# Fewer weight subtractions on GpSimd, and a hand-written VectorE order in a convolution's norm

## The chip, the cores and the metric

The kernel runs on one core of a Trainium2 chip. The metric is the device time of one execution in microseconds (us). Before the change three runs took 630.7, 631.92 and 632.24 us (median 631.92). The profile comes from one more execution, which took 633.2 us.

## The reference, cut to what matters

Two layers of a decoder trunk work on x of 256 rows x 1024, in float32. Layer 0 is an RMS norm, one projection (1024 to 3072) for two attention mixers of eight heads each, an output projection, a residual, an RMS norm and a SwiGLU feed-forward of width 2816. Layer 1 has the same frame with other mixers:

```python
gz, ca, cg = split(rms_norm(x) @ odd_w_in + odd_b_in)
gu, gv = split(gelu(gz)); gv = layer_norm(gv)      # gMLP: gv mixed over rows per group
c_out = gu * (tril(w_s) @ gv + b_s)
c = ca * sigmoid(cg)                               # Conformer convolution, 512 channels, 31 taps
c = causal_depthwise_conv(c, conv_w) + conv_b
d_out = silu(layer_norm(c))                        # the norm that the change reorders
x = x + concat(c_out, d_out) @ odd_w_out
x = x + swiglu(rms_norm(x))
```

## The kernel before, in words

**Split products.** Every float32 product is made of three TensorE passes: each operand is split into a rounded high half and the rest (low). For activations the helper `split` does it (lines 239, 240). For weights it is done once per block.

**Weight blocks.** The weights are cut into blocks of 1 MB, in the order of use: `dk dq dv mk mq mv` (two blocks of four rows of tiles each, attention's projections), `eo` (four, output projection), feed-forward 0, then layer 1: `gv` (two), `cg ca cg ca` (numbers 0, 0, 1, 1), `gu` (two), `oo` (four: 0, 2, 4, 6), feed-forward 1. A `Block` has two halves `f`. Each half takes two steps: `split_hi`, a copy on ScalarE (tile `whi`, line 133), and `split_lo`, a subtraction raw - high (tile `wlo`, line 137) on VectorE, or on GpSimd where the block was planned so. In attention these are `mv` 0, `dv` 1 and `mq` 1 (`ON_POOL`); in layer 1 `cg`, `ca`, `gu` and `oo`, except `oo` 4.

**When they are issued.** Using a block for the first time puts the steps of the one two places on into the list `todo` (`ahead`; the pair `cg`, `ca` together). `pump(n)` issues the next n steps; `tick`, called from every matmul step, pumps one at a set pace unless `held`. After the second half's `split_lo` a block calls `load_next`: SyncE's queue issues the load of the block three places on, into the raw buffer that has come free (three raw buffers, eight buffers each for high and low halves).

**Order.** TensorE runs in the order of the program. The other engines' order is set by a planner when the program is built, except inside regions opened by `in_order(...)`, where the named engines run in the order written. GpSimd's order in the convolution stage is written (`pool_order`).

**Attention.** `qk_prep` norms and rotates a projection (lines 607 to 631); a power on GpSimd (line 620) gives its factors. A unit (a pair of heads) has a start (scores, line 700; mask and maximum on VectorE, line 707; exponentials on ScalarE, 709), for the differential heads `dc` (745) and `e` (747) on VectorE, then two units later the transposes of `e` on TensorE (718), and after that the product with v (728). Projection steps fill TensorE between units.

**Norm between stages (`close`).** The last products of rows 0 to 127 (m = 0), then those of m = 1, are ended by residual (358) and sum of squares; `norm_rows` gets the factor (a power on GpSimd, 310) and scales two halves of the row (`scr`, line 331); `norm_T` transposes them on TensorE (340) and splits them. The transposes of m = 1 stand between the first steps of the next stage. Steps of the weight blocks are pumped at three places, their numbers in `SPLITS`: in the norm of m = 0, after its first transpose, and in the norm of m = 1. Entry 1 is the `close` ahead of layer 1.

**Convolution's norm.** The mean over channels is a matmul with ones (1172). Per m: `center` subtracts it (1177), squares on ScalarE (1180), sums over the four channel tiles on VectorE (1182). `scale` sums over partitions on TensorE (1188), takes the power on GpSimd (299), and makes a scaled identity `dg` (1192). `conv_out` spreads it with a matmul (1197), multiplies (1198), applies SiLU on ScalarE (1201) and splits the result into `cT` (shown as `oT` in the profile). Between them `some(n)` runs n of the sixteen ready steps of the output projection (`SOME`), and the rest runs after. The products that need the convolution's part come after that, in `close`.

Of the kernel before, what the change touches and what calls it, by code (L numbers as in the profile page):

```python
# [22 lines left out]
F32 = mybir.dt.float32  # L23
FR = mybir.dt.float32r
AF = mybir.ActivationFunctionType
ALU = mybir.AluOpType
AX = mybir.AxisListType

P = 128
# [3 lines left out]
MT = S // P  # L33
# [9 lines left out]
LOOK = 2  # L43
PACE = (3, 1, 2, 1)

ON_POOL = (('mv', 0), ('dv', 1), ('mq', 1))

WARM = (5, 4)
PUMPS = (0, 9, 7)

# [7 lines left out]
SHARES = (5, 4, 4, 5, 4, 1, 7, 5, 1, 1, 5, 4, 0, 1, 5, 0, 3, 2, 2, 7, 2)  # L58


SPLITS = ((2, 3, 7), (12, 3, 1), (7, 3, 5))
N_T0 = (5, 4, 5)
N_T1 = (10, 5, 10)


TAP_RATE = 0.55
N_DIAG = 12
SOME = (3, 4, 2, 4)
LAMBDA_INIT = 0.8 - 0.6 * math.exp(-0.3 * 0)


# [1 line left out]
def trunk_kernel(ctx: ExitStack, tc: tile.TileContext, a: dict, out: bass.AP):  # L73
    nc = tc.nc
# [11 lines left out]
    def scratch():  # L86
        return act.tile([P, 512], F32, name="scr", tag="scr", bufs=6)
# [8 lines left out]
    plan, blocks, todo = [], {}, deque()  # L96
    at_block, ticks, held, background, pace = [-1], [0], [False], [], [PACE[0]]

    class Block:


        def __init__(self, src, rows_, cols, axis, lo_engine):
            self.src, self.rows, self.cols, self.axis = src, rows_, cols, axis
            self.lo_engine = lo_engine or nc.vector
            self.per = rows_ // 2
            self.parts, self.left = [None, None], [1, 1]
            self.index, self.loaded, self.pair = len(plan), False, None
# [26 lines left out]

        def split_lo(self, f, r=slice(None)):
            hi, lo = self.half(f)
            self.lo_engine.tensor_tensor(lo[:, r], self.source(f)[:, r], hi[:, r].bitcast(F32), op=ALU.subtract)  # L137

        def split_row(self, i, lo_engine):

            f, r = i // self.per, slice(i % self.per, i % self.per + 1)
            self.split_hi(f, r)
            self.lo_engine = lo_engine
            self.split_lo(f, r)
            self.left[f] = 0
            if i == self.rows - 1:
                self.load_next()
# [25 lines left out]
    def pump(n):  # L173
        for _ in range(min(n, len(todo))):
            b, f, step = todo.popleft()
            step(f)
            if step == b.split_lo:
                b.left[f] = 0
                if f == 1:
                    b.load_next()  # L180
# [10 lines left out]
    def plan_w(key, src, k0, kn, c0, cn, axis="k", lo_engine=None):  # L191
        b = Block(src[k0 * P:(k0 + kn) * P, c0:c0 + cn].rearrange("(k p) n -> p k n", p=P), kn, cn, axis, lo_engine)
        plan.append(b)
        blocks[key] = b

    def plan_out(name, src, nk, **kw):
        for k0 in range(0, nk, 2):
            plan_w((name, k0), src, k0, 2, 0, D, **kw)

    def plan_ffn(layer):  # L200
        for j in range(FT // 2):
            for part in range(2):
                plan_w((f"f{layer}", j, part), a["ffn_w_in"][layer], 0, KT, part * FF + j * 256, 256, "c" if j else "k")
        plan_out(f"fo{layer}", a["ffn_w_out"][layer], FT)

    for name, c0 in (("dk", 512), ("dq", 0), ("dv", 1024), ("mk", 2048), ("mq", 1536), ("mv", 2560)):
        for h in range(2):
            plan_w((name, h), a["even_w_in"][0], 4 * h, 4, c0, 512, lo_engine=nc.gpsimd if (name, h) in ON_POOL else None)
    plan_out("eo", a["even_w_out"][0], KT)
    plan_ffn(0)  # L210
    for h in range(2):
# [5 lines left out]
    for j in range(2):  # L217
        plan_w(("gu", j), a["odd_w_in"][0], 0, KT, j * 256, 256, "c", lo_engine=nc.gpsimd)
    plan_out("oo", a["odd_w_out"][0], KT, lo_engine=nc.gpsimd)
    blocks["oo", 4].lo_engine = nc.vector  # L220
    plan_ffn(1)

    def passes(ps, lhs, rhs, first, last):
# [13 lines left out]
    def split(hi, lo, src):  # L237

        nc.scalar.activation(hi, src, AF.Copy)
        nc.vector.tensor_tensor(lo, src, hi.bitcast(F32), op=ALU.subtract)  # L240

    def in_order(*engines):

        region = ExitStack()
        region.enter_context(tc.manual_schedule(engines={getattr(mybir.EngineType, e) for e in engines}))
        return region
# [5 lines left out]
    ident = consts.tile([P, P], F32, name="ident")  # L252
# [26 lines left out]
    def col(name, i):  # L279
        return vec[:, rows[name] + i:rows[name] + i + 1]  # L280
# [14 lines left out]
    def rsqrt_mean(dst, ss, n, width):  # L295

        t = small.tile([P, width], F32, name="ms", tag=f"ms{width}")
        nc.vector.tensor_scalar(t, ss, 1.0 / n, EPS, op0=ALU.mult, op1=ALU.add)
        nc.gpsimd.tensor_tensor(dst, t, neg_half[:, :width], op=ALU.pow)
# [24 lines left out]
    def norm_rows(m, ss, gB, splits):  # L324

        r = row_factor(ss)
        pump(splits)
        xn = []
        for n in range(2):
            xn.append(scratch())  # L330
            nc.vector.scalar_tensor_tensor(xn[n], xs[:, m, n * 512:(n + 1) * 512], r, gB[:, n * 512:(n + 1) * 512],  # L331
                                           op0=ALU.mult, op1=ALU.mult)
        return xn

    def norm_T(m, n, xn, xT, ptag):

        pt = ptag()
        ms = slice(m * P, (m + 1) * P)
        for j in range(4):
            nc.tensor.transpose(pt[:, j * P:(j + 1) * P], xn[n][:, j * P:(j + 1) * P], ident)  # L340
        split(xT[0][:, 4 * n:4 * n + 4, ms], xT[1][:, 4 * n:4 * n + 4, ms], pt.rearrange("p (a b) -> p a b", b=P))

    def run(steps):
        for _ in steps:
            pass
# [17 lines left out]
    def tail_steps(lhs, ws, k0, m, pss, order):  # L363

        for n, k in order:
            out_step(lhs, ws[k // 2], k0 + k, k % 2, m, n, pss[m][n], False, k == 3)
            yield n, k
# [4 lines left out]
    def close(site, lhs, ws, k0, pss, gB, ptag, tail0=True):  # L372
# [5 lines left out]
        def end(m, n):  # L378
            residual(m, n, pss)
            square(m, n, ss[m])  # L380
# [9 lines left out]
        end(0, 1)  # L390
        xn0 = norm_rows(0, ss[0], gB, SPLITS[site][0])
        for i, (n, k) in enumerate(tail_steps(lhs, ws, k0, 1, pss, BY_BLOCK)):
            if i == 3 and ws[0].index + 4 < len(plan):
                plan[ws[0].index + 4].ahead()
            if i == N_T0[site]:
                norm_T(0, 0, xn0, xT, ptag)
                pump(SPLITS[site][1])
            if k == 3:
                end(1, n)
        norm_T(0, 1, xn0, xT, ptag)  # L400
        xn1 = norm_rows(1, ss[1], gB, SPLITS[site][2])

# [85 lines left out]
    with tc.tile_pool(name="attn", bufs=1) as ap, tc.tile_pool(name="pat", bufs=1, space=bass.MemoryType.PSUM) as pat:  # L488
# [242 lines left out]
        class DiffPair:  # L731
            late = LAG + 3
# [29 lines left out]
        class MobaPair:  # L762
            late = LAG + 2
# [136 lines left out]
        for m in range(MT):  # L900
            po = pat.tile([P, 512], F32, name="po", tag="po")
            r = ap.tile([P, 2, NH // 2, 2], F32, name="dr", tag="dr", bufs=2)
            units += [DiffPair(m, p, po, r) for p in range(4)]
        for m in range(MT):
            po = pat.tile([P, 512], F32, name="po", tag="po")
            r = ap.tile([P, NH // 2, 2], F32, name="mr", tag="mr", bufs=2)
# [94 lines left out]
    with tc.tile_pool(name="odd", bufs=1) as op, tc.tile_pool(name="pod", bufs=1, space=bass.MemoryType.PSUM) as pod:  # L1001
# [168 lines left out]
        def mean():  # L1170
            for i, ct in enumerate((3, 0, 1, 2)):
                nc.tensor.matmul(pm[:, :S], ones, conv[:, ct, :], start=i == 0, stop=i == 3)

        def center(m):
            ms = slice(m * P, (m + 1) * P)
            cm[m] = scratch().rearrange("p (a b) -> p a b", b=P)
            nc.vector.scalar_tensor_tensor(cm[m], pm[:, None, ms].to_broadcast([P, 4, P]), -1.0 / 512, conv[:, :, ms],
                                           op0=ALU.mult, op1=ALU.add)
            csq = scratch().rearrange("p (a b) -> p a b", b=P)
            nc.scalar.activation(csq, cm[m], AF.Square)  # L1180
            csum = scratch()[:, :P]
            nc.vector.tensor_reduce(csum, csq.rearrange("p a b -> p b a"), axis=AX.X, op=ALU.add)
            return csum

        def scale(m, csum):

            var = pm[:, S + m:S + m + 1]
            nc.tensor.matmul(var, csum, ones[:, 0:1], start=True, stop=True)
            rs = small.tile([P, 1], F32, name="cvr")
            rsqrt_mean(rs, var, 512, 1)  # L1190
            dg = scratch()[:, :P]
            nc.vector.tensor_scalar(dg, ident, rs, None, op0=ALU.mult)
            return dg

        def conv_out(m, dg):
            ms = slice(m * P, (m + 1) * P)
            nc.tensor.matmul(pb[:, ms], ones, dg, start=True, stop=True)
            nc.vector.tensor_tensor(cm[m], cm[m], pb[:, None, ms].to_broadcast([P, 4, P]), op=ALU.mult)
            dT = scratch().rearrange("p (a b) -> p a b", b=P)
            for ct in range(4):  # L1200
                nc.scalar.activation(dT[:, ct, :], cm[m][:, ct, :], AF.Silu, scale=col("cln_g", ct), bias=col("cln_b", ct))
            split(cT[0][:, 4:, ms], cT[1][:, 4:, ms], dT)
# [15 lines left out]
        def some(n):  # L1218
            for _ in range(n):
                next(part)  # L1220

        some(SOME[0])
        mean()
        csum = [center(m) for m in range(MT)]
        some(SOME[1])
        dg = [scale(0, csum[0])]
        some(SOME[2])
        dg.append(scale(1, csum[1]))
        conv_out(0, dg[0])
        some(SOME[3])  # L1230
        conv_out(1, dg[1])
        run(part)
        pool_order.close()
        ws = [blocks["oo", k0] for k0 in (4, 6)]
# [65 lines left out]
```

## Time and profile before

| | |
|---|---|
| profiled execution | 633.2 us; span of its instructions 631.4 us |
| TensorE matmul busy | 609.0 us, 96% of the span |
| weight load on TensorE (beside matmuls) | 517.6 us, 82% |
| VectorE busy | 421.1 us, 67% |
| ScalarE busy | 345.7 us, 55% |
| GpSimd busy | 121.7 us, 19% |
| `wlo` on VectorE, line 137 | 166 instructions, 206.3 us |
| `wlo` on GpSimd, line 137 | 26 instructions, 62.9 us |
| DMA | 104.32 MB, mean 165 GB/s |
| granted TensorE clock, mean | 0.989 |

How to read it: an engine's busy time is the sum of its instructions; an instruction that is held up while it runs counts as busy. The granted clock is a share of full speed; 1.00 is 2.4 GHz, 0.50 is 1.2 GHz. "idle before <- releaser" names the instruction that ended last among those that were waited for. Times in windows and timelines count from the start of the span.

### The profile page before, as it was taken

The numbers are of one execution on the slowest core, as the hardware profiler recorded it, in microseconds if no ns is written. First come the engines' busy times: TensorE is split into PE (matmuls) and PEld (weight loads), VectorE is DVE, ScalarE is ACT, GpSimd is POOL, SyncE is SP. The second block draws the span as 40 slices with busy tenths as digits, with TensorE's granted clock in tenths as the row PEclk, the third lists the DMA queues.
The fourth block names the chain that finished last, engine by engine and source line by source line (L and its number), as shares of the span: only waits on it lengthen the run. The fifth ranks groups of instructions, "written<-read, shape, count | busy, mean of one in ns | idle before, by whom it ended". The sixth has DMA issues, their size and how long they took to land.

```text
span 631.4 us, 8906 instructions
## 1 busy us (share of the span) xinstructions
PE 609.0 (96%) x3420; PEld 517.6 (82%) x3420; DVE 421.1 (67%) x710; ACT 345.7 (55%) x621; POOL 121.7 (19%) x97
## 2 busy tenths in 40 slices
PE   7989799999999999999998999988999999999997
PEld 5867577787988888888886899867988888888886
DVE  3799998547666648664446389986766666665431
ACT  5764686555655587553446775446455555554320
POOL 1998321101000000000003695550000000000000
PEclk9999799999999999999999799999999999999999
DMA  7855424224766437555552553225656555555401
GB/s 248 308 196 175 158 106 132 70 66 149 245 225 215 146 128 266 185 168 185 199 197 67 167 199 134 68 89 178 208 193 201 196 174 173 193 199 190 145 0 67
DMA packets 72791, 104.32 MB, mean 165 GB/s; under 512 B 3068, under 2 KB 56492, under 8 KB 72748
## 3 DMA queue, kind: packets, MB, share of 16 engines
q1 hardware_dynamic: 72748, 103.74, 49.5%
q8 instruction: 27, 0.44, 0.3%
q14 instruction: 16, 0.13, 0.1%
HBM read 102.69 MB, written 1.05 MB: 164 GB/s over the span
## 4 chain that ended last, share of the span: by engine, by line
PE 52%; issue 29%; DVE 11%; POOL 3%; ACT 2%; DMA 1%; SPq 1%; POOLq 0%; DVEq 0%; ACTq 0%
PE mm L233 15%; PE mm L225 8%; PE mm L227 8%; PE mm L234 8%; PE mm L226 8%; DVE wlo L137 3%; DVE scr L331 2%; PE tq L700 1%; DMA raw<-in_even_w_in 1%; POOL rm L310 1%; DVE t L627 1%; PE po L728 1%; ACT whi L133 1%; DVE t L621 1%; PE tq L718 1%
## 5 line engine op out<-in xcount | busy, mean ns | idle before, releaser
L133 ACT ACTIVATE whi<-raw 128x1024 fp32r<-128x1024 f32 (+1 forms) x192 | 197.7, 1040 | 175.7 <-PE mm L233 80.1
L137 DVE TENSOR_TENSOR wlo<-raw,whi 128x1024 fp32r<-128x1024 f32 (+1 forms) x166 | 206.3, 1248 | 124.5 <-ACT whi L133 122.9
L233 PE MATMUL mm<-xT,whi 128*128 128x512 f32 x640 | 226.8, 399 | 0.0
L234 PE MATMUL mm<-xT,wlo 128*128 128x256 f32 x640 | 179.7, 281 | 0.0
L233 PEld LDWEIGHTS mm<-xT,whi 128*128 128x128 f32 x640 | 120.2, 188 | 29.6 <-issue 0.2
L234 PEld LDWEIGHTS mm<-xT,wlo 128*128 128x128 f32 x640 | 120.9, 189 | 0.0
L225 PE MATMUL mm<-whi,xT 128*128 128x512 f32 (+1 forms) x176 | 68.2, 387 | 0.6 <-ACT xT L545 0.5
L137 POOL TENSOR_TENSOR wlo<-raw,whi 128x1024 fp32r<-128x1024 f32 (+1 forms) x26 | 62.9, 2439 | 19.7 <-ACT whi L133 19.6
L227 PE MATMUL mm<-whi,hT_lo 128*128 128x512 f32 (+1 forms) x176 | 66.5, 378 | 0.0
L226 PE MATMUL mm<-wlo,hT_hi 128*128 128x512 f32 (+1 forms) x176 | 66.5, 378 | 0.0
L225 PE MATMUL mm<-whi,hT_hi 128*128 128x512 f32 (+1 forms) x176 | 66.4, 378 | 0.0
L227 PE MATMUL mm<-whi,xT 128*128 128x512 f32 (+1 forms) x176 | 64.1, 364 | 1.1 <-DVE xT L240 1.1
L226 PE MATMUL mm<-wlo,xT 128*128 128x512 f32 (+1 forms) x176 | 64.3, 366 | 0.5 <-DVE wlo L137 0.5
L310 POOL TENSOR_TENSOR rm<-st,neg_half 128x1 f32<-128x1 f32 x8 | 7.1, 894 | 188.9 <-DVE st L308 188.9
L225 PEld LDWEIGHTS mm<-whi,xT 128*128 128x128 f32 x176 | 34.5, 196 | 7.8 <-issue 1.6
L227 PEld LDWEIGHTS mm<-whi,xT 128*128 128x128 f32 x176 | 34.6, 196 | 6.8 <-DVE xT L240 1.8
L226 PEld LDWEIGHTS mm<-wlo,xT 128*128 128x128 f32 x176 | 34.7, 197 | 4.8 <-DVE wlo L137 1.3
L225 PEld LDWEIGHTS mm<-whi,hT_hi 128*128 128x128 f32 x176 | 33.1, 188 | 6.4
L226 PEld LDWEIGHTS mm<-wlo,hT_hi 128*128 128x128 f32 x176 | 33.1, 188 | 6.4
L227 PEld LDWEIGHTS mm<-whi,hT_lo 128*128 128x128 f32 x176 | 33.0, 188 | 6.4
L464 DVE TENSOR_TENSOR scr<-mm,scr 128x256 f32<-128x256 f32 x80 | 33.2, 418 | 5.8 <-ACT scr L463 5.7
L1077 DVE SCALAR_TENSOR_TENSOR cv<-cpad,cw,cv 128x256 f32<-128x256 f32 x87 | 35.7, 481 | 0.2
(226 smaller groups left out, 868.6 us busy)
## 6 DMA issues: line engine op xcount, KB each, us to landing
raw<-in_ffn_w_in SPq DMA_DIRECT2D x44, 1024.0 KB
raw<-in_ffn_w_out SPq DMA_DIRECT2D x22, 1024.0 KB
raw<-in_even_w_in SPq DMA_DIRECT2D x10, 1024.0 KB
raw<-in_odd_w_in SPq DMA_DIRECT2D x8, 1024.0 KB
raw<-in_even_w_out SPq DMA_DIRECT2D x4, 1024.0 KB
raw<-in_odd_w_out SPq DMA_DIRECT2D x4, 1024.0 KB
xs<-in_x SPq DMA_DIRECT2D x4, 256.0 KB
raw<-in_even_w_in SPq DMA_DIRECT2D x4, 256.0 KB
```

Of the source, the lines that this page charges most:

```text
L133: nc.scalar.activation(self.half(f)[0][:, r], self.source(f)[:, r], AF.Copy)
L137: self.lo_engine.tensor_tensor(lo[:, r], self.source(f)[:, r], hi[:, r].bitcast(F32), op=ALU.subtract)
L225: nc.tensor.matmul(ps, lhs[0], rhs[0], start=first, stop=False)
L226: nc.tensor.matmul(ps, lhs[0], rhs[1], start=False, stop=False)
L227: nc.tensor.matmul(ps, lhs[1], rhs[0], start=False, stop=last)
L233: nc.tensor.matmul(bank, w[0], x[2][:, k, :, :].rearrange("p a b -> p (a b)"), start=k == 0, stop=False)
L234: nc.tensor.matmul(bank[:, :S], w[1], x[0][:, k, :], start=False, stop=k == KT - 1)
L310: nc.gpsimd.tensor_tensor(r, t[:, 1:2], neg_half[:, :1], op=ALU.pow)
L331: nc.vector.scalar_tensor_tensor(xn[n], xs[:, m, n * 512:(n + 1) * 512], r, gB[:, n * 512:(n + 1) * 512], op0=ALU.mult, op1=ALU.mult)
L464: nc.vector.tensor_tensor(s, bank[:, :S], s, op=ALU.add)
L621: nc.vector.scalar_tensor_tensor(t1v, psv, rx[m], c, op0=ALU.mult, op1=ALU.mult)
L1077: nc.vector.scalar_tensor_tensor(conv[:, ct, :] if t == TAPS - 1 else acc, cpad[:, ct, t:t + S], cw[:, t, ct:ct + 1], acc, op0=ALU.mult, o ...
```

## The change

The list `ON_POOL` goes: all attention blocks subtract on VectorE. A block now has one engine for each half; of `cg` 0 and `ca` 0 the second half goes to VectorE. `SPLITS` entry 1 pumps one step more after the first transpose and none in the norm of m = 1. In the convolution's norm VectorE runs in the order written; both `center` come before both sums; `dg` is made on ScalarE; the SiLU and the split are a function of their own, called after both products; the high halves of `oo` 4 and 6 are issued ahead of the norm and their low halves at set places (`oo` 4 on VectorE, `oo` 6 on GpSimd).

```diff
-ON_POOL = (('mv', 0), ('dv', 1), ('mq', 1))
...
-SPLITS = ((2, 3, 7), (12, 3, 1), (7, 3, 5))
+SPLITS = ((2, 3, 7), (12, 4, 0), (7, 3, 5))
...
-SOME = (3, 4, 2, 4)
+SOME = (3, 4, 1, 2, 1)
...
-            self.lo_engine = lo_engine or nc.vector
+            self.lo_engine = [lo_engine or nc.vector] * 2
...
-            self.lo_engine.tensor_tensor(lo[:, r], self.source(f)[:, r], hi[:, r].bitcast(F32), op=ALU.subtract)
+            self.lo_engine[f].tensor_tensor(lo[:, r], self.source(f)[:, r], hi[:, r].bitcast(F32), op=ALU.subtract)
...
-            plan_w((name, h), a["even_w_in"][0], 4 * h, 4, c0, 512, lo_engine=nc.gpsimd if (name, h) in ON_POOL else None)
+            plan_w((name, h), a["even_w_in"][0], 4 * h, 4, c0, 512)
...
-    blocks["oo", 4].lo_engine = nc.vector
+    for b in (blocks["cg", 0], blocks["ca", 0]):
+        b.lo_engine[1] = nc.vector
+    blocks["oo", 4].lo_engine = [nc.vector] * 2
...
             nc.scalar.activation(csq, cm[m], AF.Square)
+            return csq
+
+        def summed(csq):
             csum = scratch()[:, :P]
...
-            nc.vector.tensor_scalar(dg, ident, rs, None, op0=ALU.mult)
+            nc.scalar.activation(dg, ident, AF.Copy, scale=rs)
...
             nc.vector.tensor_tensor(cm[m], cm[m], pb[:, None, ms].to_broadcast([P, 4, P]), op=ALU.mult)
+
+        def conv_silu(m):
+            ms = slice(m * P, (m + 1) * P)
             dT = scratch().rearrange("p (a b) -> p a b", b=P)
...
+        late = [blocks["oo", k0] for k0 in (4, 6)]
+        for b in late:
+            for f in range(2):
+                b.left[f] = 2
+                b.split_hi(f)
+
+        def low(b, f):
+            b.split_lo(f)
+            b.left[f] = 0
+            if f == 1:
+                b.load_next()
+
+        order = in_order("DVE")
         some(SOME[0])
         mean()
-        csum = [center(m) for m in range(MT)]
+        low(late[0], 0)
+        low(late[1], 0)
+        csq = [center(m) for m in range(MT)]
+        csum = [summed(c) for c in csq]
         some(SOME[1])
         dg = [scale(0, csum[0])]
         some(SOME[2])
         dg.append(scale(1, csum[1]))
+        some(SOME[3])
         conv_out(0, dg[0])
-        some(SOME[3])
+        some(SOME[4])
         conv_out(1, dg[1])
+        low(late[0], 1)
+        low(late[1], 1)
+        for m in range(MT):
+            conv_silu(m)
+        order.close()
         run(part)
```

## Rows read from the trace of the kernel before

**Rows 1.** Windows: us, busy PE, PEld, DVE, ACT, POOL (instructions); clock, DMA, GB/s.
```profile
31.20:63.50 32.30, 30.43 (x148) 23.53 (x146) 32.30 (x53) 17.46 (x30) 29.01 (x10) 1.00 0.55 186
63.50:67.14 3.64, 0.04 (x2) 0.00 (x1) 3.57 (x5) 1.46 (x3) 3.18 (x2) 1.00 0.57 230
67.14:74.50 7.36, 7.36 (x25) 5.75 (x26) 7.32 (x29) 5.22 (x17) 1.64 (x1) 0.54 0.37 142
...
85.00:97.00 12.00, 11.98 (x75) 9.27 (x76) 12.00 (x37) 9.74 (x27) 2.74 (x2) 1.00 0.26 88
...
344.95:347.80 2.85, 0.10 (x2) 0.03 (x1) 2.85 (x2) 1.40 (x5) 2.85 (x2) 0.96 0.00 0
347.80:354.40 6.60, 6.29 (x23) 5.18 (x24) 4.56 (x4) 3.95 (x12) 4.85 (x2) 0.50 0.39 111
...
415.10:422.10 7.00, 5.34 (x24) 3.89 (x24) 5.39 (x9) 2.09 (x3) 4.17 (x4) 1.00 0.49 152
422.10:427.20 5.10, 3.14 (x13) 2.13 (x14) 5.10 (x5) 3.79 (x8) 1.63 (x1) 1.00 0.46 141
```
**Rows 2.** TensorE's waits, whole span: us in total, times, longest us.
```profile
PE tq L718 <- DVE e L747: 3.6, 1, 3.6
PE cv L340 <- DVE scr L331: 3.1, 2, 2.7
PE mm L227 <- DVE oT_lo L240: 1.9, 1, 1.9
```
**Rows 3.** Timeline of GpSimd in attention: start us, us, instruction.
```profile
32.10 5.93 POOL L137 TENSOR_TENSOR wlo<-raw,whi 128x1024 fp32r<-128x1024 f32 x2
...
52.02 5.36 POOL L137 TENSOR_TENSOR wlo<-raw,whi 128x1024 fp32r<-128x1024 f32 x2
...
61.53 5.14 POOL L137 TENSOR_TENSOR wlo<-raw,whi 128x1024 fp32r<-128x1024 f32 x2
```
**Rows 4.** Timeline of VectorE in attention.
```profile
31.22 4.56 DVE L137 TENSOR_TENSOR wlo<-raw,whi 128x1024 fp32r<-128x1024 f32 x2
...
52.70 2.35 DVE L873 TENSOR_TENSOR lsum<-lexp 128x1 f32<-128x1 f32 x1
...
55.05 3.41 DVE L137 TENSOR_TENSOR wlo<-raw,whi 128x1024 fp32r<-128x1024 f32 x1
...
62.24 2.23 DVE L627 TENSOR_TENSOR t<-t,rsh 128x512 f32<-128x512 f32 x1
...
64.60 2.10 DVE L745 SCALAR_TENSOR_TENSOR dc<-sums,neg_lam,dr 128x2 f32<-128x2 f32 x1
...
80.38 0.18 DVE L743 RECIPROCAL dr<-sums 128x4 f32<-128x4 f32 x1 [1.09 <-ACT e L709]
```
**Rows 5.** Single lines, whole span: duration ns min/median/max, first and last start us.
```profile
L137 DVE TENSOR_TENSOR wlo<-raw,whi x166: 678/1226/3429, 6.1 to 606.9; 128x1024 fp32r<-128x1024 f32 x160, 128x512 fp32r<-128x512 f32 x6
L627 DVE TENSOR_TENSOR t<-t,rsh x4: 680/1462/2271, 36.3 to 74.2; 128x512 f32<-128x512 f32 x4
L745 DVE SCALAR_TENSOR_TENSOR dc<-sums,neg_lam,dr x8: 211/214/2099, 64.6 to 104.1; 128x2 f32<-128x2 f32 x8
L616 DVE TENSOR_REDUCE ssh<-scr x8: 668/675/686, 28.2 to 86.7; 128x16 f32<-128x512 f32 x4, 128x8 f32<-128x512 f32 x4
L929 ACT ACTIVATE diag<-ident,cw x62: 384/388/403, 225.4 to 367.5; 128x128 fp32r<-128x128 f32 x62
```
**Rows 6.** Timeline of GpSimd and VectorE in the norm ahead of layer 1.
```profile
344.76 7.89 POOL L137 TENSOR_TENSOR wlo<-raw,whi 128x1024 fp32r<-128x1024 f32 x3
...
344.83 5.59 DVE L331 SCALAR_TENSOR_TENSOR scr<-xs,rm,gB 128x512 f32<-128x512 f32 x2 [0.74 <-POOL rm L310]
```
**Rows 7.** Timeline of GpSimd and VectorE in the convolution's norm.
```profile
419.00 4.74 POOL L137 TENSOR_TENSOR wlo<-raw,whi 128x1024 fp32r<-128x1024 f32 x2
...
419.06 2.41 DVE L1192 TENSOR_SCALAR scr<-ident,cvr 128x128 f32<-128x128 f32 x1 [0.66 <-POOL cvr L299]
421.99 3.95 DVE L137 TENSOR_TENSOR wlo<-raw,whi 128x1024 fp32r<-128x1024 f32 x2
```

More of the change, by code (lines that the diff above doesn't have):

```diff
@@ L142, in split_row @@
             self.split_hi(f, r)
-            self.lo_engine = lo_engine
+            self.lo_engine[f] = lo_engine
             self.split_lo(f, r)
```

## Prediction

> **What bounds the kernel now.** I read the page first: TensorE is busy 96% of the span, so only its idle stretches and its granted clock can give time back. Cutting the span into equal windows puts nearly all idle time outside the first and last 20 us into three places: attention, the norm in front of layer 1, and the convolution's norm. TensorE's own waits name who was late: VectorE's `e` (3.6 us at once), VectorE's normed rows of line 331 (3.1 in two waits, 2.7 of it at once), VectorE's split of the convolution's output (1.9) [rows 2]. Finer windows give the prices [rows 1]. Attention: idle 32.30 - 30.43 = 1.9 us in 31.2 to 63.5, then 3.6 us. Right behind that the granted clock is 0.54 over 7.36 us, that is, mostly at the lower level of 1.2 GHz. Work done at 0.54 costs 7.36 x 0.46 = 3.4 us more than at 2.4 GHz. Norm of layer 1: idle 344.95 to 347.80, then 0.50 over 6.60 us: 3.1 us more for its 6.29 us of work. Convolution's norm: idle (7.00 - 5.34) + (5.10 - 3.14) = 3.6 us between 415.1 and 427.2; no fall of the clock is seen behind it.
>
> Then I asked why VectorE is late. In attention it is busy 32.30 of 32.30 us and 12.00 of 12.00 in 85 to 97: it is the second bound there. But some of its instructions are far too long, and these lie beside GpSimd's `wlo` subtractions: GpSimd has pairs at 32.10, 52.02 and 61.53 [rows 3]; VectorE shows, in those stretches, a pair of subtractions of 4.56, a 128x1 one (line 873) of 2.35, one of 3.41, one of 2.23, one of 2.10 [rows 4]. The same lines when free: 1.23 (median), 0.68, 0.21 [rows 5]. The reduction of line 616 never exceeds 0.69 [rows 5]. So it is instructions with two inputs in SBUF that wait until GpSimd's subtraction ends; those with one do not. In the norm the two line-331 instructions take 5.59 together, beside three GpSimd subtractions from 344.76 that take 7.89 [rows 6].
>
> The Trainium skill says the same ("SBUF — State Buffer", section "Who interferes with whom"): VectorE and GpSimd share one port pair under an exclusive lock, and a VectorE instruction with two SBUF inputs waits for a whole GpSimd instruction that reads SBUF, and the reverse. The trace agrees (2.10 against 0.21). What speaks against the change in that rule is weighed below.
>
> **Part 1, attention: `ON_POOL` goes.** Six half-block subtractions move from GpSimd to VectorE. Added on VectorE: 6 x 1.23 = 7.4 us. Removed there, over the free duration: the pair 4.56 - 2.46 = 2.1; line 627 at its longest 2.27 - 0.68 = 1.6; the 128x1 one 2.35 - 0.21 = 2.1; 3.41 - 1.23 = 2.2; 2.23 - 0.68 = 1.5; 2.10 - 0.21 = 1.9 [rows 4, 5]. Sum 11.4. Net 4.0 less work for VectorE. The last two (3.4 us) stand directly in front of the `e` for which TensorE idles 3.6, and the first pair of additions stands in place of the first blocked pair, so the large wait should go. What is late next: VectorE, which is full until 97. TensorE can use its 8.9 us (1.9 + 3.6 + 3.4) only as far as VectorE keeps up, and that is 4.0 plus idle time that closes up. One such piece is the 1.1 us that VectorE waited for ScalarE's exponentials at 80.4 [rows 4], which come earlier when TensorE does. I take 5.1. Bounds: 8.9 if VectorE's deferrable subtractions give way to the urgent steps, and below, 1.7 if the leftover 3.8 us of waiting falls in one place and the clock falls again (5.1 - 3.4). GpSimd keeps only the small powers here, which no longer queue behind a subtraction. SyncE's loads follow the last subtraction of a block; VectorE's free subtraction takes about half of GpSimd's, so they are not issued later for that.
>
> **Part 2, norm of layer 1.** The second halves of `cg0` and `ca0` go to VectorE, and `SPLITS[1]` puts all four steps of the first halves behind the first transpose, none behind the second norm's factor. So GpSimd runs nothing beside the second pair of line-331 instructions. Each then takes about 0.7 (line 627, also 128x512 with two SBUF inputs). The first was ready to start at 344.83 [rows 6], so TensorE's transpose starts near 345.6 instead of 347.80: 2.2 us. The second wait (3.1 - 2.7 = 0.4 [rows 2]) goes too. With the long wait gone I expect no fall: 3.1 us. Sum 5.7, less 0.1 for the splits behind: 5.6. Hidden costs: 2 x 1.23 more on VectorE after the norm's steps, where it was busy only 4.56 of 6.60 us, partly blocked [rows 1]. The moved first half of `ca0` now runs beside the first norm and may hold one instruction there for one subtraction (7.89 / 3 = 2.6 us); both line-331 instructions of that norm stand before it or take turns, so I take nothing. Bounds: 2.6 (clock falls all the same, 5.7 - 3.1) and 6.0.
>
> **Part 3, convolution's norm.** Four things. (a) Both centerings now come before both reductions, so the variance matmul waits for the reduction alone. (b) The scaled identity moves to ScalarE: about 0.39 there, as line 929 [rows 5], against 2.41 for the one that stood beside GpSimd's pair from 419.00 [rows 7]. (c) VectorE had two subtractions of the next blocks (3.95 from 421.99, one of them blocked [rows 7]) in front of the second product and the split; by hand these now come later, and both products precede any subtraction. (d) `SOME` cuts the spare matmul steps 3, 4, 1, 2, 1, leaving five behind the second product, to cover the SiLU and the split. Moving (b) frees VectorE of 2.41, moving (c) of 3.95 before a split for which TensorE waited 1.9: all 3.6 of idle time is reachable. I take 3.2, leaving 0.4 for the two hand-overs of (a) to GpSimd's power and ScalarE.
>
> What counts against it: `oo` 6 stays on GpSimd and its second half runs where VectorE has `oo` 4's second half and then the first split of `oT`, both with two SBUF inputs.
>
> By the skill's rule above the split may be held for one whole GpSimd subtraction; with it this part would give 3.2 - 2.4 = 0.8 (half of the 4.74 [rows 7]).
>
> From the rows alone: a held pair took 4.56 against 2.46, so the price is 2.1 at most, and the five spare steps stand in front of it; I keep 1.1 to 3.6 for this part. The four high halves of `oo` 4 and 6 are now issued just ahead of the norm instead of in passing; if ScalarE does them late, the hand-written order holds VectorE's whole queue (centerings, reductions, products, for which TensorE waits) behind the first low half. Four copies in a row before the squares would cost the 3.2 and no more than about as much again: part 3 from -3.2. The loads that follow `oo` 4 and 6 on SyncE are issued only after the second low halves; the tail's sixteen matmul steps lie between them and their use, so I take nothing. Without that cover it costs up to 6 us, from the start of the idle windows, 415.1, to about 421, where I expect the last low half by the order written (an estimate).
>
> **Sum.** 5.1 + 5.6 + 3.2 = 13.9. The profiled execution took 633.2 us (span 631.4 and 1.8 around it): 619.3. It lies 1.3 above the median of the runs, 631.92, so 618.0 is forecast.
>
> **Rivals.** First, VectorE keeps up in attention. Part 1 gives 8.9, part 3 all of 3.6: 633.2 - 18.1 - 1.3 = 613.8. For it: not every subtraction is needed as soon as it can run. Against: VectorE full in 85 to 97.
> Second, the clock falls again, or the hand order waits. Part 1 gives 1.7: 621.4. With part 3 at nothing as well: 624.6. For it: VectorE remains the second bound and 3.8 us of TensorE's waiting stay somewhere in attention. Against: 3.6 us of idle time, none of it over 1.96 at once, brought no fall at 415 to 427.
> Third, on the other side: the long VectorE instructions are not GpSimd's doing (they wait for their inputs, say the exponentials or `rs`), so the change doesn't do what it says: slower. Place: VectorE's full queue in attention. Price: the 7.4 us of added subtractions, with parts 1 and 2 giving nothing back: 631.9 + 7.4 - 3.2 = 636.1. It decides when less than a fourth of the lengthening goes away: 7.4 - 3.2 = 4.2, against 11.4 + 5.6 = 17.0. Against: six of six blocked stretches end with a GpSimd subtraction, and a 128x2 instruction of 2.10 is 0.21 elsewhere.
>
> **How the numbers follow.** Forecast (615.5 to 620) 0.45; VectorE keeps up (below) 0.21; clock or hand order (620 to 628) 0.23; not GpSimd's doing 0.07; two of these together, near no change 0.04. The range that leaves out two in ten is 612.8 to 626.5, which takes in the bounds of parts 1 and 3 singly; the forecast's own is 615.5 to 620. Within 0.3% (1.9 us, about what a measurement can tell from no change) lies 630.0 to 633.8. Faster 0.87, the same 0.05, slower 0.08.
>
> **What would show it.** In the profile after: no VectorE line 627, 745 or 873 above 1 us, nor 331 in the norm of m = 1; no row of GpSimd `wlo` in 30 to 70; TensorE's wait for `e` under 1 us at any one place, and small waits for `e` at later units; clock 1.00 in the windows that now have 0.54 and 0.50; the wait for the rows of line 331 under 0.8 at once; idle time in the convolution's norm under 1 us; line 1192 on ScalarE. It is wrong if VectorE's instructions keep their lengths, if either fall of the clock is still there, or if TensorE waits for a load or for `wlo` behind the convolution.

## The result, and the profile after

The changed kernel takes 616.2 us (median of four runs, 615.33 to 616.42), the kernel before on the same chip 632.08 (630.7 to 632.71): the ratio is 0.9753, interval 0.9733 to 0.9773. The forecast was 618.0, so it came out 1.8 us faster than that. The profiled execution took 616.31 us, its span is 614.6.

The page's slices for TensorE and its granted clock, each digit one fortieth of the span:

```profile
PE   7989999999999999999999999999999999999997
PEclk9999999999999999999999999999999999999999
```

TensorE is now busy 600.3 us, 98% of the span, and no slice shows a lower clock. Where the time came from can be read matmul by matmul, since both kernels issue the same 3420: the difference of the starts grows by 0.75 us in the first microseconds (start-up, which differs from run to run), by 6.8 in attention, 0.8 in feed-forward 0 (whose blocks of matmuls ran a little slower in the execution before; see the last section), 4.4 in the norm ahead of layer 1 and 4.0 up to the end of the convolution's norm. That is 16.8 in all, and 15.2 in the three places that were forecast (13.9 there). The expectations of runs 1 and 3 go by 6.9 and 4.1 for two of these.

TensorE's waits after, whole span (total us, times, longest), which answer [rows 2]:

```profile
PE tq L638 <- DVE t L627: 1.7, 2, 1.1
PE cv L340 <- DVE scr L331: 1.6, 1, 1.6
...
PE tq L718 <- DVE e L747: 0.4, 1, 0.4
```

The 3.6 us for `e` have become 0.4, the 3.1 for the normed rows 1.6, and the 1.9 for the convolution's split is gone. What is left at the head of the list is VectorE's rotated tile `t`, 1.1 us at once.

**Attention.** Windows over VectorE's queue from the first wave of subtractions to the last `e`, first before, then after (us, busy PE, PEld, DVE, ACT, POOL, then clock, DMA, GB/s):

```profile
31.20:106.30 75.10, 69.21 (x362) 54.01 (x361) 72.31 (x175) 48.40 (x112) 39.72 (x15) 0.95 0.42 142
```
```profile
30.45:98.95 68.50, 65.78 (x363) 51.73 (x361) 66.72 (x181) 47.77 (x112) 18.70 (x9) 1.00 0.44 153
85.00:97.00 12.00, 11.38 (x72) 9.37 (x70) 10.64 (x33) 8.11 (x24) 1.64 (x1) 1.00 0.27 87
```

The stretch is 6.6 us shorter. VectorE's work in it fell by 72.31 - 66.72 = 5.6, though it has six instructions more, and its idle time from 2.8 to 1.8. The clock is 1.00 throughout. VectorE is full no longer in 85 to 97: 10.64 of 12.00. The steps that filled it there before run some 7.5 us earlier now, and in 77.5 to 89.5 it is busy 10.64 of 12.00 as well. Its timeline in the places of [rows 4]:

```profile
30.47 4.62 DVE L135 TENSOR_TENSOR wlo<-raw,whi 128x1024 fp32r<-128x1024 f32 x4
...
35.61 0.68 DVE L627 TENSOR_TENSOR t<-t,rsh 128x512 f32<-128x512 f32 x1
...
57.81 0.68 DVE L627 TENSOR_TENSOR t<-t,rsh 128x512 f32<-128x512 f32 x1
...
59.94 0.22 DVE L745 SCALAR_TENSOR_TENSOR dc<-sums,neg_lam,dr 128x2 f32<-128x2 f32 x1
```

Four subtractions now take what two took (4.62 against 4.56), line 627 has 0.68 where it had 2.27 and 2.23, and line 745 has 0.22 where it had 2.10.

**The norm ahead of layer 1.** GpSimd's timeline, then VectorE's, which answer [rows 6]:

```profile
328.63 5.21 POOL L135 TENSOR_TENSOR wlo<-raw,whi 128x1024 fp32r<-128x1024 f32 x2 [0.71 <-ACT whi L131]
333.79 0.19 POOL L1051 MEMSET cpad<- 128x120 f32 x1
335.98 1.42 POOL L310 TENSOR_TENSOR rm<-st,neg_half 128x1 f32<-128x1 f32 x1 [2.00 <-DVE st L308]
```
```profile
335.68 0.15 DVE L308 TENSOR_SCALAR st<-st 128x1 f32<-128x1 f32 x1
335.76 1.23 DVE L135 TENSOR_TENSOR wlo<-raw,whi 128x1024 fp32r<-128x1024 f32 x1
337.43 1.41 DVE L331 SCALAR_TENSOR_TENSOR scr<-xs,rm,gB 128x512 f32<-128x512 f32 x2 [0.45 <-POOL rm L310]
```

The pair of line 331 takes 1.41 in place of 5.59. But a subtraction of VectorE (335.76) now stands between the mean square and the factor, and the factor's power on GpSimd takes 1.42: it ends at 337.40, 0.4 behind the end of that subtraction (336.99). TensorE still waits 1.6 us. The windows behind [rows 1]'s two of this place:

```profile
337.00:338.40 1.40, 0.07 (x1) 0.10 (x2) 0.97 (x2) 1.21 (x5) 0.40 (x1) 1.00 1.04 366
338.40:345.00 6.60, 6.60 (x51) 6.29 (x52) 2.43 (x4) 6.00 (x17) 0.09 (x1) 1.00 0.88 298
```

The 6.60 us behind the wait run at 1.00, 51 matmuls where 23 ran at 0.50.

**The convolution's norm.** Windows of its two halves, and VectorE's timeline ([rows 1, 7] before):

```profile
397.67:402.30 4.63, 4.63 (x22) 3.62 (x20) 3.72 (x5) 2.30 (x4) 4.02 (x4) 1.00 0.00 0
402.30:410.50 8.20, 8.03 (x38) 6.17 (x38) 5.52 (x9) 6.28 (x14) 4.29 (x4) 1.00 0.31 96
```
```profile
405.46 0.69 DVE L1201 TENSOR_TENSOR scr<-scr,cv 128x512 f32<-128x512 f32 x1 [1.56 <-PE cv L1200]
406.79 0.69 DVE L1201 TENSOR_TENSOR scr<-scr,cv 128x512 f32<-128x512 f32 x1 [0.64 <-PE cv L1200]
407.40 2.35 DVE L135 TENSOR_TENSOR wlo<-raw,whi 128x1024 fp32r<-128x1024 f32 x2
409.67 0.68 DVE L240 TENSOR_TENSOR oT_lo<-scr,oT_hi 128x512 fp32r<-128x512 f32 x1
```

TensorE idles 0.2 us where it idled 3.6. VectorE waits for TensorE now, not the other way round, and its subtractions follow both products.

### The profile page after: what moved, and what is told of

It reads as the page before. It is cut to its first block, busy times and chain, and to the rows that moved or that the text cites. A ratio compares the mean times of both kernels' runs of the same rounds, so it can differ in the third digit from the quotient of the medians.

```text
span 614.6 us, 8908 instructions
## 1 busy us (share of the span) xinstructions
PE 600.3 (98%) x3420; PEld 512.3 (83%) x3420; DVE 409.7 (67%) x716; ACT 345.9 (56%) x623; POOL 96.7 (16%) x89
## 5 line engine op out<-in xcount | busy, mean ns | idle before, releaser
L135 DVE TENSOR_TENSOR wlo<-raw,whi 128x1024 fp32r<-128x1024 f32 (+1 forms) x174 | 210.1, 1213 | 123.4 <-ACT whi L131 121.8
L225 PE MATMUL mm<-whi,xT 128*128 128x512 f32 (+1 forms) x176 | 66.0, 375 | 0.4 <-ACT xT L545 0.4
L227 PE MATMUL mm<-whi,xT 128*128 128x512 f32 (+1 forms) x176 | 63.0, 358 | 1.2 <-DVE xT L240 1.1
L226 PE MATMUL mm<-wlo,xT 128*128 128x512 f32 (+1 forms) x176 | 62.6, 355 | 0.0
L135 POOL TENSOR_TENSOR wlo<-raw,whi 128x1024 fp32r<-128x1024 f32 (+1 forms) x18 | 41.3, 2331 | 21.9 <-ACT whi L131 21.9
L227 PEld LDWEIGHTS mm<-whi,xT 128*128 128x128 f32 x176 | 33.6, 191 | 7.1 <-DVE xT L240 2.0
L225 PEld LDWEIGHTS mm<-whi,xT 128*128 128x128 f32 x176 | 33.6, 191 | 6.9 <-issue 1.3
```

What stands on the lines that cost most here:

```text
L135: self.lo_engine[f].tensor_tensor(lo[:, r], self.source(f)[:, r], hi[:, r].bitcast(F32), op=ALU.subtract)
L225: nc.tensor.matmul(ps, lhs[0], rhs[0], start=first, stop=False)
L226: nc.tensor.matmul(ps, lhs[0], rhs[1], start=False, stop=False)
L227: nc.tensor.matmul(ps, lhs[1], rhs[0], start=False, stop=last)
```

## The experiments

The theory: a GpSimd subtraction holds any VectorE instruction that reads two operands from SBUF until it ends, and the reverse. Where VectorE's queue is full, the lengthening arrives at the next urgent step; when TensorE idles for it, the clock falls, and that costs about as much again. Rivals: only the subtraction directly in front of the first `e` matters; or it is GpSimd's being busy at all, not its reading; or the parts don't add up. Edits are of the changed kernel unless another is named; added lines shift the line numbers by a few. Not all ran on one chip, so each time stands with its ratio to the kernel before on the same chip (its medians there: 630.29 to 631.7).

**1. Attention's subtractions back on GpSimd.**

```diff
+ON_POOL = (('mv', 0), ('dv', 1), ('mq', 1))
...
+            plan_w((name, h), a["even_w_in"][0], 4 * h, 4, c0, 512, lo_engine=nc.gpsimd if (name, h) in ON_POOL else None)
```

> The changed kernel with only attention's six subtractions back on GpSimd. Theory (a GpSimd subtraction holds every VectorE instruction with two SBUF inputs): the matmul-by-matmul difference of the two traces puts 6.9 us of the gain before the end of attention, so 616.2 + 6.9 = 623 us (621.5 to 624.5), with VectorE's instructions of 2 us and more and a stretch at half clock back in attention, and the norm of layer 1 as in the changed kernel. Rival (attention gained by the planner's new order, or the gain came later): 616 to 618.5, or long VectorE instructions without a fall of the clock.

622.47 us (621.6 to 623.74), ratio 0.9865 (0.9844 to 0.9885). By the matmuls it is 6.7 us behind the changed kernel, all of it by the end of attention: 0.3 in start-up, 6.3 in attention. The long VectorE rows are back to the hundredth (4.56, 2.35, 3.41, 2.23, 2.10), and so are the wait for `e`, 3.6, and the stretch behind it at 0.53, mostly at 1.2 GHz:

```profile
62.50:66.30 3.80, 0.21 (x2) 0.01 (x1) 3.73 (x5) 1.62 (x4) 3.34 (x2) 1.00 0.57 229
66.30:73.50 7.20, 7.20 (x25) 5.63 (x26) 7.16 (x29) 5.06 (x17) 1.64 (x1) 0.53 0.38 146
```

Part 1 alone makes this difference; behind attention the two kernels run alike.

**2. The norm ahead of layer 1 as before.**

```diff
-SPLITS = ((2, 3, 7), (12, 4, 0), (7, 3, 5))
+SPLITS = ((2, 3, 7), (12, 3, 1), (7, 3, 5))
...
-    for b in (blocks["cg", 0], blocks["ca", 0]):
-        b.lo_engine[1] = nc.vector
```

> The changed kernel with only the norm ahead of layer 1 as before (second halves of cg 0 and ca 0 on GpSimd, SPLITS entry 1 as before). Theory: line 331 is held by GpSimd again, TensorE waits some 2.7 us and its clock falls: 616.2 + 4.4 = 620.6 us (619.5 to 621.8). Rival (the fall needs the earlier fall or another phase): the wait comes back without a fall, 617.2 to 618.2.

619.63 us (618.42 to 622.21), ratio 0.9832 (0.9804 to 0.986); by the matmuls it loses 4.9 at this norm. The pair of line 331 takes 5.60 again beside three GpSimd subtractions, and the clock falls behind it:

```profile
335.40:338.50 3.10, 0.33 (x3) 0.07 (x2) 3.02 (x2) 1.60 (x6) 3.10 (x3) 1.00 0.00 0
338.50:345.50 7.00, 5.89 (x25) 4.88 (x26) 4.53 (x4) 4.38 (x14) 4.81 (x2) 0.56 0.44 128
```

At 0.56 the 5.89 us of work cost 2.6 more than at 2.4 GHz; the rest is the wait.

**3. The convolution's norm as before** (its order, `SOME`, `dg` on VectorE, high and low halves in passing).

```diff
-SOME = (3, 4, 1, 2, 1)
+SOME = (3, 4, 2, 4)
...
-            nc.scalar.activation(dg, ident, AF.Copy, scale=rs)
+            nc.vector.tensor_scalar(dg, ident, rs, None, op0=ALU.mult)
...
-        order = in_order("DVE")
...
```

> The changed kernel with only the convolution's norm as before (planner's order, centering and sum per half, scaled identity on VectorE, SOME as before; oo 6 on GpSimd in both). Theory: all of the 4.1 us that the traces show there come back: 620.3 us (619.3 to 621.3), no fall of the clock. Rival (part of it was luck of the order that the other edits changed): under 618.5.

622.62 us (621.02 to 624.08), ratio 0.9865 (0.984 to 0.989): some 2 us longer than expected. By the matmuls it loses 6.2 here, 4.5 of it waits (1.9 for the split, 1.4 for the centering, and smaller ones). The other 1.7 is this:

```profile
409.00:416.00 7.00, 4.22 (x19) 2.70 (x18) 7.00 (x7) 4.18 (x9) 3.15 (x2) 1.00 0.37 124
416.00:420.50 4.50, 4.50 (x14) 3.53 (x13) 3.13 (x4) 2.52 (x5) 0.00 (x0) 0.62 0.92 289
```

Behind these waits the clock fell for 3.4 us here, where the kernel before, with 3.6 us of idle time in the same place, shows no fall [rows 1]. So whether it falls behind waits of this kind is not settled by their sum. Nor is it the same in every execution of one kernel: over the four executions of run 3 the mean granted clock was 1.000 once (621.02 us, inside the range expected), 0.997 twice and 0.994 once (624.08). And the three parts don't add up exactly: undone singly they cost 6.3, 4.9 and 6.2 by the matmuls, 17.4 against 15.2 together, this fall being 1.7 of the difference.

**4 and 5. The second low halves behind the norm.** They are written behind the norm's last split; in 4 with the second high halves in front of the first low halves, in 5 behind them. Of 5:

```diff
+                if site == 1:
+                    for _ in range(4):
+                        todo.pop()
...
+                if site == 1:
+                    for b in plan[ws[0].index + 4].pair:
+                        b.split_hi(1)
...
+            if site == 1:
+                for b in plan[ws[0].index + 4].pair:
+                    b.split_lo(1)
+                    b.left[1] = 0
+                    b.load_next()
```

> The changed kernel with the second low halves of cg 0 and ca 0 written behind the norm's last split instead of left to the planner. Theory (the 1.55 us that TensorE still waits for line 331 come from the subtraction that the planner put in front of the norm's factor, which also holds the power on GpSimd, 1.42 instead of 0.55): wait down to 0.5, 616.2 - 1.1 = 615.1 us. Rival (the wait is the chain residual, square, factor itself): no change, 616.2.

> As e4_late_halves, but the second high halves are issued behind the first ones, so that GpSimd's two subtractions stay where they are in the changed kernel (in e4 they moved back to 331.7 to 336.5 and held the power for the norm's factor in GpSimd's queue: 1.7 us of VectorE's waiting). Theory (the wait of 1.55 us for line 331 is made by a subtraction in front of the factor, VectorE's in the changed kernel, GpSimd's in e4): the power runs at its 0.55, TensorE's wait falls to about 0.6, 615.2 us. Rival (the wait is the chain of residual, square and factor itself): wait 1.5 and 616.2.

4 took 616.0 us (614.78 to 617.47), ratio 0.9762 (0.974 to 0.9783), and still waits 1.7: GpSimd's own pair moved to 331.71, and its power now queues behind that. 5 took 615.4 (613.74 to 615.53), ratio 0.9758 (0.9734 to 0.9781). GpSimd's power and TensorE's wait in 5:

```profile
336.07 0.56 POOL L310 TENSOR_TENSOR rm<-st,neg_half 128x1 f32<-128x1 f32 x1 [1.82 <-DVE st L308]
```
```profile
PE cv L340 <- DVE scr L331: 0.7, 1, 0.7
```

With no subtraction beside it the power takes 0.56, and the wait falls from 1.6 to 0.7, as the prediction had it for the changed kernel ("under 0.8 at once"). The 0.9 us are seen at the spot only; by the times the two kernels can't be told apart.

**6. GpSimd busy with fills that read nothing.** Four fills of 128x512 for each of the six moved subtractions, the subtractions staying on VectorE.

```diff
+            if any(blocks.get(key) is self for key in ON_POOL):
+                for _ in range(4):
+                    nc.gpsimd.memset(idle[0], 0.0)
```

> The changed kernel, in which GpSimd fills an unused tile (24 fills of 128x512, about 12 us in all) where its attention subtractions were issued in the kernel before; VectorE's order is the same as in the changed kernel. Theory (what holds VectorE is that GpSimd reads SBUF through a shared way): VectorE's subtractions beside the fills stay at 1.2 us and the time at 616 to 617, with only the powers behind the fills later. Rival (any GpSimd work of that length holds VectorE): subtractions of 2 us and more beside the fills, 618 to 621.

619.59 us (619.3 to 620.49), ratio 0.9832 (0.9807 to 0.9858). GpSimd's timeline, then VectorE's beside it:

```profile
31.24 9.33 POOL L140 MEMSET idle_tile<- 128x512 f32 x16
40.53 4.47 POOL L628 TENSOR_TENSOR rsh<-msh,neg_half 128x16 f32<-128x16 f32 x1
```
```profile
30.38 4.62 DVE L141 TENSOR_TENSOR wlo<-raw,whi 128x1024 fp32r<-128x1024 f32 x4
...
35.52 0.68 DVE L635 TENSOR_TENSOR t<-t,rsh 128x512 f32<-128x512 f32 x1
...
38.83 0.60 DVE L626 TENSOR_SCALAR msh<-ssh 128x16 f32<-128x16 f32 x1
...
45.03 0.69 DVE L635 TENSOR_TENSOR t<-t,rsh 128x512 f32<-128x512 f32 x1 [2.20 <-POOL rsh L628]
```

Four subtractions beside the fills take 4.62, as in the changed kernel without them, and line 627's counterpart 0.68. So a GpSimd that only writes holds none of the instructions with two inputs in SBUF; for these it must read. It is not without any effect: line 626 here, a small scaling of one input in SBUF, took 0.60, 0.44 and 0.36 us beside fills, where 0.17 is usual. The time is lost another way, which the expectation had left out: the fills stand in front of the power (40.53) in GpSimd's queue, `t` is 2.20 late, TensorE waits 3.4 us and the clock is 0.54 in 44 to 51. The total, taken alone, would have spoken for the rival.

**7. Only `mv` 0 on GpSimd; 10. only `dv` 1 and `mq` 1.**

```diff
+ON_POOL = (('mv', 0),)
```
```diff
+ON_POOL = (('dv', 1), ('mq', 1))
```

> The changed kernel with only mv 0's two subtractions back on GpSimd (the pair that stood in front of the first e). Theory (place decides: the hold falls on the urgent steps): TensorE waits 2 to 3.5 us for the first e again, with the stretch at half clock: 619.5 to 622.5, most of what all six cost (623). Rival (VectorE's total load decides): two of the six cost a third, 618 to 618.6, no fall of the clock.

> The changed kernel with four of the six attention subtractions back on GpSimd (second blocks of dv and mq), those of mv 0 left on VectorE, so that none of GpSimd's pairs is meant to stand in front of the first e. Theory (load and place: each held VectorE instruction costs its lengthening wherever VectorE is full): VectorE saves 4 x 1.23 = 4.9 and is lengthened by about 8.0, so attention ends about 3.1 later, 618 to 619.5, with a wait of about 1.4 more for t of line 627 and perhaps a fall of the clock. Rival (only the pair in front of the first e matters): 616 to 617.

7 took 620.67 us (619.96 to 622.18), ratio 0.9843 (0.9813 to 0.9873). The planner set the two subtractions apart, at 55.61 and 60.03; beside them VectorE shows

```profile
56.32 2.24 DVE L626 TENSOR_TENSOR t<-t,scr 128x512 f32<-128x512 f32 x1
...
60.09 2.88 DVE L629 TENSOR_TENSOR t<-t,rsh 128x512 f32<-128x512 f32 x1 [0.72 <-POOL rsh L622]
```

TensorE waits for `e` twice, 1.2 and 1.1 us, and the clock is 0.54 in 82.5 to 90. The time is as expected, though through two short waits, not the one of 2 to 3.5. By the matmuls it loses 4.6 in attention.

10 took 622.04 us (620.14 to 622.8), ratio 0.9844 (0.9818 to 0.9871), 2.5 above the theory's upper figure and far from the rival's. By the matmuls attention costs 4.1 over the changed kernel, which puts it 0.8 above; start-up and feed-forward 0, which the edit leaves alone, differ by another 0.8 each between the two executions. No GpSimd subtraction stands in 57 to 75, and yet (VectorE's timeline, TensorE's waits, the window):

```profile
52.25 2.35 DVE L875 TENSOR_TENSOR lsum<-lexp 128x1 f32<-128x1 f32 x1
...
54.60 3.42 DVE L137 TENSOR_TENSOR wlo<-raw,whi 128x1024 fp32r<-128x1024 f32 x1
...
65.14 0.60 DVE L749 SCALAR_TENSOR_TENSOR e<-e,dc 128x128 f32<-128x128 f32 x2
```
```profile
PE tq L720 <- DVE e L749: 2.8, 2, 2.5
...
PE tq L640 <- DVE t L629: 1.4, 1, 1.4
```
```profile
62.00:70.00 8.00, 5.51 (x26) 4.03 (x25) 8.00 (x26) 6.45 (x20) 1.64 (x1) 0.82 0.72 280
```

What was held at 52 to 58 arrives at `e` at 65.14, through a queue that is full in between; the wait is 2.5 us and a shorter fall follows. So the place directly in front of `e` is not needed. Nor do the pieces add: by the matmuls in attention the two cost 4.6 us, the four 4.1, and all six 6.3, where the sum would be 8.7. In these runs, once VectorE was late enough for a wait and a fall of the clock, what was added cost less.

**8. The planner's order in the convolution's norm**, all else of part 3 kept.

```diff
-        order = in_order("DVE")
...
-        order.close()
```

> The changed kernel without the hand-written VectorE order in the convolution's norm; the placed low halves, both centerings first, the identity on ScalarE, SOME and the late SiLU stay. The planner then puts two low halves ahead of the centerings and one between the two products. Theory (the order matters as each of these is 1.2 to 2.4 us in front of an urgent step): 1.5 to 3 us slower, 617.7 to 619.2. Rival (the other edits of this part carry the gain): 616 to 617.

618.76 us (617.78 to 621.86), ratio 0.9825 (0.9792 to 0.9858). At the norm it loses 1.3 us by the matmuls; its TensorE is busy 6.84 us of 402.3 to 410.5, where the changed kernel has 8.03, and waits 0.8 for the reduction. By the trace the order by hand is worth 1.3 of the part's 4.0, which leaves 2.7 to the other edits together. They were not taken apart further, so what each of them gives is not shown. The time is 2.6 above the changed kernel's median, more than the trace accounts for.

**9. `dv` 1's subtractions behind the next preparation**, on the kernel of 5.

```diff
-PUMPS = (0, 9, 7)
+PUMPS = (0, 5, 11)
```

> Built on the kernel in which the second low halves of cg 0 and ca 0 are written behind the norm's last split (615.4 us). Here, in the first norm and its neighbourhood, the pumps are set to 0, 5, 11, so that the low halves of dv 1 stand behind the preparation of the next projection instead of in front of it. Theory (VectorE's subtractions in front of an urgent step cost TensorE the wait): the 1.1 us that TensorE waits for the row tile t of line 627 near 35 us goes, about 614.4. Rival (VectorE's queue is full there anyway, so the subtractions only move in front of another urgent step, or the projection that uses dv 1 waits for them): 615.4 or more.

615.92 us (615.2 to 616.55), ratio 0.9749 (0.9726 to 0.9772). The wait for `t` near 35 us is gone, and in its place stands one for the subtraction itself:

```profile
38.31 0.50 PE L226 MATMUL mm<-wlo,xT 128*128 128x512 f32 x1 [1.53 <-DVE wlo L135]
```

The rival was right: TensorE waits for a subtraction instead, and nothing was gained.

## Why the prediction was right

**Bounds.** That VectorE's lateness, not TensorE's work, was what could be taken away held in all three places; all 3420 matmuls are still there, and the waits and falls are what went.

**The mechanism** held. Every held row that the change was to free is short again; attention's come back with the subtractions to the hundredth (run 1), and stay short beside fills that read nothing (run 6). One hold was left in place: the pair of line 331 in the norm of m = 0 takes 3.62 beside GpSimd's subtractions, before and after. With that the third rival (not GpSimd's doing, 636.1) falls. One half-sentence of it was wrong, "those with one do not": it was read from the reduction of line 616 alone. The scaled identity of line 1192 has one tensor and one factor per row as inputs, and took 2.41 beside GpSimd's pair [rows 7] where the other of the two took 0.28; in run 6 a scaling of one input was lengthened even beside fills. The rule that the prediction cites from the Trainium skill ("SBUF — State Buffer", section "Who interferes with whom") agrees in both directions: GpSimd's power took 1.42 beside a VectorE subtraction and 0.56 without (run 5). It did not show for GpSimd's powers as the one that holds, though they read SBUF too: in run 6 a VectorE subtraction that began at 48.49, beside a power that ran from 47.77 to 50.67, took its usual 1.22.

**Part 1** was too small: 5.1 against 6.8. The 11.4 us of lengthening went as worked out. The step that was mis-sized is "Added on VectorE: 6 x 1.23 = 7.4 us": the stretch holds five more subtractions, not six (31 subtractions of VectorE up to the last `e`, 26 in the kernel before), and the sixth runs behind that `e`. 5 x 1.22 - 11.4 = -5.3, and -5.6 was measured. The idle time that closed was 1.0, forecast 1.1. Of the small waits for `e` at later units, which were to remain, only 0.4 us is there. The gain lies almost half way from the forecast to the first rival (VectorE keeps up, 8.9), held back by `t` (1.7) and, as run 9 shows, by a queue that is still full around 35 us.

**Part 2** was too large: 5.6 against 4.4. The fall's 3.1 came back in full. The step that failed is the price of the wait (2.2 + 0.4): 1.5 came, and the wait of 1.6 is the sign that the prediction missed (it named under 0.8 at once). The prediction set the splits of the second halves "behind"; the planner put one between the mean square and the factor, and there VectorE held GpSimd. The hold was looked for in one direction only. Run 5 gets 0.9 of it back at the spot.

**Part 3** was a little small: 3.2 against 4.0 by the matmuls, 3.4 by the idle time. The hand-overs were given 0.4 and took 0.2. The sentence that weighed a hold of the split by GpSimd's last subtraction didn't come to pass: that one ran from 404.50 to 406.89, ahead of VectorE's pair at 407.40. The high halves were not late, and no wait of TensorE for a load or for `wlo` lies behind the convolution.

**The second rival's** ground was right in kind: what the clock does behind short waits can't be told from their length. Before, 3.6 us of idle time brought no fall; in run 3 waits of the same kind (4.5 in all) brought one, and in run 7 one came with the second of two waits of 1.2 and 1.1 us. In the changed kernel a single wait of 1.6 brought none, and the mean granted clock was 1.000 in all four executions.

**The total** is nearer than its parts: errors of +1.7 and +0.8 against -1.2 cancel to 1.3 of the miss of 1.8, which is luck. Start-up and feed-forward 0 differ by another 1.6 between the two profiled executions, which no part claims; the 1.3 that the forecast took off, since the profiled execution before lay above the median, stands against it.

## What to carry to other kernels

Moving work to an idle engine is not free when both read SBUF: look for instructions whose largest duration is many times their median, and see what the other engine runs beside them, in both directions. A full queue carries a hold over 10 us to the next urgent step, and in the profiled executions each single wait of 2.5 to 3.6 us for VectorE (before, and runs 1, 2, 6, 10) was followed by a spell at half clock that cost 1.7 to 3.4 us more. So the first microseconds of lateness cost the most here; behind shorter waits a spell came in some runs and not in others. Where a planner sets the order, a step freed of one engine may be put in front of the next urgent one; read where it landed before counting the gain.

## What the runs showed of the hardware that was not expected

- GpSimd's 128x1 power is held too: 1.42 us where it began beside a VectorE subtraction of 128x1024, 0.56 else. Its 128x16 power took 4.47 where it began beside one (run 6, 40.53) and 2.90 where one began after it (47.77).
- Sixteen GpSimd fills (9.33 us) held no VectorE instruction with two inputs in SBUF, but a scaling of one input took up to 0.60 beside them, 0.17 else.
- Spells at the lower clock come in two lengths here: about 7 us (before, and runs 1, 2, 6, 7) and 3.4 us (runs 3 and 10, costing 1.7 each). Nothing in the runs says which will follow a given wait, and executions of one kernel differ: run 10's four had mean granted clocks from 0.995 (622.8 us) to 1.000 (620.14).
- The feed-forward's blocks of 48 matmuls took 8.48 us in some executions and 8.32 in others, whatever the kernel (before and after in feed-forward 0; after and run 2 in feed-forward 1, where it made 1.9 us). Differences below 2 us were read from the traces, not from the times alone.
